# Sliding-window attention: score matmuls over 64 rows of the array, two heads beside each other, in place of 128-row matmuls over stacked high and low parts

## The chip, the cores and the metric

One core of one Trainium2 chip runs the whole program. The metric is device time in microseconds (us) of that core, from the program's start to its end. All times of the profile are microseconds unless a column says ns.

## The reference

The program computes a two-layer decoder trunk for 1024 tokens of width 1024. Layer 0 mixes tokens with a gated linear recurrence, layer 1 with sliding-window attention; each is followed by a gated feed-forward net with a short convolution. The change lies in the attention: 16 query heads and 4 key/value heads of width 64, a window of 128 tokens, a learned sink for each head and a relative-position bias. Cut to that:

```python
def swa_sink_mixer(h, k, v, w_q, sinks, bias, mask, w_out):
    q = (h @ w_q).reshape(B, nb, SW_WINDOW, SW_KV_HEADS, SW_GROUP, SW_HEAD_DIM)
    kk, vv = with_prev(k), with_prev(v)          # blocks [j-1, j]: 256 keys for 128 queries
    logits = jnp.einsum('bntgrd,bnsgd->bngrts', q, kk) * SW_HEAD_DIM ** -0.5
    logits = jnp.where(mask, logits + bias, -jnp.inf)
    m = jnp.maximum(logits.max(-1), sink)
    p = jnp.exp(logits - m[..., None])
    denom = p.sum(-1) + jnp.exp(sink - m)
    o = jnp.einsum('bngrts,bnsgd->bntgrd', p, vv)
    return (o / denom).reshape(B, S, D) @ w_out
```

The `einsum` of the third line, queries by keys over 64 numbers, is the operation whose form changes.

## The kernel before

**High and low parts.** Nearly every matmul works on numbers that are split in two: a high part (the value as the array's fast 32-bit format, `F32R`, holds it) and a low part (the value less the high part). A product is then three matmuls: high by high, high by low, low by high. `mm3` (L172 to L174) writes these three; with its column of `psmm` or `psax`, both in PSUM, it makes most of the program. ScalarE (ACT) makes a high part by a copy, VectorE (DVE) a low part by a subtraction.

**The attention stage.** It begins when the first layer's feed-forward net ends. `k_part` projects the shared keys, `v_part` the values. Heads are worked in eight pairs `c`; the two heads `e` of a pair belong to neighbouring key heads. `q_unit(c)` loads the query weights of a pair (through a ring of raw tiles, `load`, L138, and a ring of six slots of the tile `HL`), `q_proj` projects them in two halves of 512 tokens, and `q_split` takes each half out of PSUM, scaled by 0.125. `attend(c, bp, q)` then does four steps `bp` for a pair, each of two blocks `jj` of 128 queries and both heads: scores, mask and bias, softmax, transposes, values. That makes 32 calls.

**Scores before.** A head has width 64, half of the array's 128 rows. The kernel fills the rows with both parts. `K` holds for each head 64 rows of the high part and, in the other 64 partitions, its low part (`k_part` writes the low part across, L1140). The query's high part stands twice, in both halves of the partitions (tile `q`), and its low part once, with zeros in the other half (`QB`, in slot 5 of `HL`, whose zeros are set at L1307). One 128-row matmul of the doubled high part then gives high by high plus high by low, a second with the low part gives low by high: two matmuls for each head and block (L1208), eight in a call, each with 128x128 weights of its own and 256 columns of keys streamed (128 for the first block). They write `psax`, head 0 in one PSUM bank, head 1 in the other.

**The transfers.** ACT and DVE write the two parts into a raw tile (`place["ML"]`, L1191 and L1192), which is thereby taken out of the ring of three, and six DMAs on SyncE's queue (L1196) carry the 64-row halves to their places. There are 16 such halves, and so 96 DMAs, 64 into `q` and 32 into `HL`.

**Order.** In the attention, the order on TensorE (PE), ACT, DVE and GpSimd (POOL) is that of the code; the SyncE queue (SP) is filled by a scheduler. The main loop (L1325 to L1357) is a pipeline written by hand: in each turn PE does the scores of call n, the values product (L1251, L1253) and the transposes of earlier calls, and two pieces of the next pair's `q_proj` as filler. After them DVE and ACT work on softmax while PE goes on.

Of the kernel before, what the change touches and what calls it, by code (L numbers as in the profile page):

```python
# [10 lines left out]
F32 = mybir.dt.float32  # L11
F32R = mybir.dt.float32r
U8 = mybir.dt.uint8
AF = mybir.ActivationFunctionType
ALU = mybir.AluOpType

P = 128
# [68 lines left out]
def trunk(ctx: ExitStack, tc: tile.TileContext, a: dict, out: bass.AP):  # L86
    nc = tc.nc
# [38 lines left out]
    ring = {"hl": 4, "raw": 0}  # L126
    tail, place = {}, {}
# [4 lines left out]
    def hl_at(i):  # L132
        return HL[:, 2048 * i:2048 * (i + 1)].rearrange("p (h n) -> p h n", h=2)
# [2 lines left out]
        return hl_at(j // 2)[:, j % 2, :]  # L136

    def load(loads):  # L138
        raw = tail["raw"][ring["raw"] % len(tail["raw"])]
        ring["raw"] += 1  # L140
        for view, src in loads(raw):
            nc.sync.dma_start(view, src)
        return raw
# [54 lines left out]
    def split(hi, lo, src, eng=None):  # L198
        nc.scalar.copy(hi, src)  # L199
        return low_part(lo, src, hi, eng)  # L200

    def split_scaled(hi, lo, src, scale):
        nc.scalar.activation(hi, src, AF.Copy, scale=scale)
        nc.vector.scalar_tensor_tensor(lo, src, scale, hi.bitcast(F32), op0=ALU.mult, op1=ALU.subtract)
# [461 lines left out]
    with tc.tile_pool(name="t", bufs=1, reuse_waits="tile") as raws, hgrn_pool as hp:  # L666
# [40 lines left out]
        with tc.tile_pool(name="ep", bufs=1, reuse_waits="tile") as ep:  # L707
# [50 lines left out]
            ps = psmm()  # L758
# [315 lines left out]
        ps = psax()  # L1074
# [25 lines left out]
    with (tc.tile_pool(name="ta", bufs=1, reuse_waits="tile") as raws,  # L1100
          tc.tile_pool(name="at", bufs=1, reuse_waits="tile") as at):
        raw_tail(raws)
        K = at.tile([P, 2, 2, S], F32R, name="K")
        QB = [hl_at(5)[:, i, :].rearrange("p (e t) -> p e t", e=2) for i in range(2)]
        tri = at.tile([P, P], F32, name="tri")
        nc.scalar.dma_start(tri, a["tri"])
        sk = at.tile([P, 16], F32, name="sk")
# [23 lines left out]
        def k_part(half):  # L1131
            ts = slice(half * 512, (half + 1) * 512)
            for c in range(2):
                ps = psmm()
                proj_T(khl[c], half, ps)
                heads = [(slice(64 * e, 64 * e + 64), slice(64 - 64 * e, 128 - 64 * e)) for e in range(2)]
                for e, (es, os) in enumerate(heads):
                    nc.scalar.copy(K[es, c, e, ts], ps[es])
                for e, (es, os) in enumerate(heads):
                    nc.vector.tensor_tensor(K[os, c, e, ts], ps[es], K[es, c, e, ts].bitcast(F32), op=ALU.subtract)  # L1140


        def v_part(tp):
# [20 lines left out]
        def q_unit(c):  # L1164
            bias_load(c)
            pp, r = divmod(c, 4)
            ring["hl"] = (2, 3, 4, 0, 1, 2, 3, 4)[c]
            hl = unit(lambda t: [(t.rearrange("p (k g e) -> p k g e", k=KC, g=2)[:, :, g, :],
                                  wq[:, :, 8 * pp + 4 * g + r, :]) for g in range(2)], lows)
            return hl.rearrange("p h (k c) -> p h k c", k=KC)  # L1170

        def q_proj(hl):
            qs, done = [], []
            yield qs, done
            for half in range(2):
                q = at.tile([P, 2, 512], F32R, name="q", bufs=3), QB[half]
                qs.append(q)
                ps = psmm()
                for kc in range(KC):
                    mm3(ps, lambda i: hl[:, i, kc, :], lambda i: T[:, i, kc, half * 512:(half + 1) * 512],  # L1180
                        kc == 0, kc == KC - 1)
                    od.tick()
                    if kc % 2 == 1 and kc < KC - 1:
                        yield
                done.append((q, ps))
                yield

        def q_split(q, ps):
            qh, ql = q
            M, L = [place["ML"][:, 512 * i:512 * i + 512] for i in range(2)]  # L1190
            nc.scalar.activation(M.bitcast(F32R), ps, AF.Copy, scale=0.125)  # L1191
            nc.vector.scalar_tensor_tensor(L.bitcast(F32R), ps, 0.125, M, op0=ALU.mult, op1=ALU.subtract)  # L1192
            for e in range(2):
                es, os = slice(64 * e, 64 * e + 64), slice(64 - 64 * e, 128 - 64 * e)
                for dst, src in ((qh[es, e, :], M), (qh[os, e, :], M), (ql[es, e, :], L)):
                    nc.sync.dma_start(dst.bitcast(F32), src[es])  # L1196

        def attend(c, bp, q):
            pp, r = divmod(c, 4)
            ps = psax()  # L1200
            pv = ps.rearrange("p (e j s) -> p e j s", e=2, j=2)
            for jj in range(2):
                j = 2 * bp + jj
                lo = P if j == 0 else 0
                qs, ks = slice((j % 4) * P, (j % 4 + 1) * P), slice((j - 1) * P + lo, (j + 1) * P)
                for e in range(2):
                    for part in range(2):
                        nc.tensor.matmul(pv[:, e, jj, lo:], q[bp // 2][part][:, e, qs], K[:, pp, e, ks],  # L1208
                                         start=part == 0, stop=part == 1)
            XS = at.tile([P, 2, 2, 144], F32, name="X", bufs=4)  # L1210
            X, XS = XS[:, :, :, :P], XS[:, :, :, :P + 1]
            nc.scalar.copy(X, pv[:, :, :, P:])
            nc.gpsimd.tensor_copy(XS[:, :, :, P], sk[:, 8 * pp + r:8 * pp + r + 5:4].unsqueeze(2).to_broadcast([P, 2, 2]))
            yield
            j0 = 1 if bp == 0 else 0
            for e in range(2):
                nc.vector.copy_predicated(X[:, e, j0:, :], msk[:, 7 * BL:].unsqueeze(1).to_broadcast([P, 2 - j0, P]),
                                          pv[:, e, j0:, :P])
                if j0:
                    nc.gpsimd.affine_select(out=X[:, e, 0, :], in_=X[:, e, 0, :], compare_op=ALU.is_ge,  # L1220
                                            fill=NEG, base=0, pattern=[[-1, P]], channel_multiplier=1)
            bv = bfs[c]
            nc.gpsimd.tensor_tensor(X, X, bv.unsqueeze(2).to_broadcast([P, 2, 2, P]), op=ALU.add)
            yield
            nm = sm.tile([P, 2, 2], F32, name="nm")
            dn = sm.tile([P, 2, 2], F32, name="dn")
            nc.vector.tensor_reduce(nm, XS, axis=mybir.AxisListType.X, op=ALU.max, negate=True)
            for e in range(2):
                for jj in range(2):
                    nc.scalar.activation(XS[:, e, jj, :], XS[:, e, jj, :], AF.Exp, bias=nm[:, e, jj:jj + 1],  # L1230
                                         accum_out=dn[:, e, jj:jj + 1])
            yield
            nc.vector.reciprocal(dn, dn)
            nc.vector.tensor_tensor(X, X, dn.unsqueeze(3).to_broadcast([P, 2, 2, P]), op=ALU.mult)
            yield
            pt = psmm()
            for i in range(4):
                tr(pt[:, i * P:(i + 1) * P], X[:, i // 2, i % 2, :])
            yield
            W = W0 if bp % 2 else Y[:, NB - 1, :].rearrange("p (k g s) -> p k g s", k=2, g=4)  # L1240
            nc.vector.tensor_tensor(W[:, 0], pt.rearrange("p (g s) -> p g s", g=4),
                                    tri.unsqueeze(1).to_broadcast([P, 4, P]), op=ALU.mult)
            nc.scalar.copy(W[:, 1], pt.rearrange("p (g s) -> p g s", g=4))
            yield
            po = psmm()
            for jj in range(2):
                j = 2 * bp + jj
                for e in range(2):
                    kvc = (2 * pp + e) * 64
                    o = po[64 * e:64 * e + 64, jj * P:(jj + 1) * P]  # L1250
                    mm32(o, Vt[:, max(j - 1, 0), kvc:kvc + 64], W[:, 1, 2 * e + jj, :], stop=j == 0)  # L1251
                    if j:
                        mm32(o, Vd[:, j - 1, kvc:kvc + 64], W[:, 0, 2 * e + jj, :], start=False)  # L1253
            if c < 7:
                nc.scalar.copy(Y[:, c, bp * 256:(bp + 1) * 256], po[:, :256])
            else:
                ts = slice(bp * 256, (bp + 1) * 256)
                split(T[:, 0, c, ts], T[:, 1, c, ts], po[:, :256], lows)
            yield
# [34 lines left out]
        with tc.manual_schedule(engines={EN.PE, EN.Activation, EN.DVE, EN.Pool}):  # L1294
# [9 lines left out]
            hl = q_unit(0)  # L1304
            make_lows()
            k_part(1)
            for e in range(2):  # L1307
                nc.gpsimd.memset(hl_at(5).rearrange("p i (e t) -> p i e t", e=2)[64 - 64 * e:128 - 64 * e, :, e, :]
                                 .bitcast(F32), 0.0)
            g = q_proj(hl)  # L1310
            q, done = next(g)
            hl = q_unit(1)
            make_lows()
            place["ML"] = tail["raw"][ring["raw"] % 3]
            tail["raw"] = [t for t in tail["raw"] if t is not place["ML"]]
            for _ in g:
                while done:
                    q_split(*done.pop(0))
# [97 lines left out]
```

## Time and profile before

| | us |
|---|---|
| median of 3 runs | 2199.43 (2193.86 to 2200.97) |
| the profiled execution, its own time | 2199.59 |
| its span in the trace | 2197.8 |
| PE busy | 2156.2 (98%) |
| DVE busy | 1743.4 (79%) |
| ACT busy | 926.8 (42%) |

The profiled execution's own time is 1.8 us over its span, and 0.2 us over the median of the runs. A matmul's bar in the trace is longer than the time by which it delays the next: matmuls are pipelined, and 256 columns that show as 283 ns follow each other closer than that. So the distance from start to start is read here, not the bar. PEld are the weight loads, which run beside matmuls.

### The profile page before, as it was taken

Reading aid. Unit: us, or ns where it says so; the run is one execution under the profiler, and the core shown is the slowest. Engines: PE = TensorE matmul, PEld = TensorE weight load, DVE = VectorE, ACT = ScalarE, POOL = GpSimd, SP = SyncE. Lnnn points to the kernel's source line nnn. Section 1 sums busy time; section 2 is a strip of 40 time slices with the busy share of each in tenths; the row PEclk is TensorE's granted clock in tenths of the full one; section 3 lists DMA queues with packets and bytes.
Section 4 is the critical chain, followed back from the end, with each engine's and each line's share of the span. In section 5 each row is a group of like instructions: output and inputs, shape, how many; then the busy total and the mean of one; then the engine's idle time right before and its main releaser. Section 6 shows DMA issues by size and latency. Waiting matters only on the chain.

```text
span 2197.8 us, 33422 instructions
## 1 busy us (share of the span) xinstructions
PE 2156.2 (98%) x13135; PEld 1815.5 (83%) x13135; DVE 1743.4 (79%) x2295; ACT 926.8 (42%) x1577; POOL 187.3 (9%) x209
## 2 busy tenths in 40 slices
PE   8999999999999999999999999999999999999998
PEld 7888888978888888887888888878888888887887
DVE  3777665565789988888998766657899988889987
ACT  4333333332744443344344346655644444443431
POOL 0221111120100000000000122211000000000001
PEclk9999999999999999999999999999999999999999
DMA  5554443252222222238854354433123222259563
GB/s 198 193 192 173 154 173 116 64 126 90 87 84 86 85 82 87 86 103 268 281 169 133 105 145 108 111 118 118 68 96 106 86 77 77 78 168 318 187 212 135
DMA packets 239623, 293.68 MB, mean 134 GB/s; under 512 B 31513, under 2 KB 162282, under 8 KB 236650
## 3 DMA queue, kind: packets, MB, share of 16 engines
q1 hardware_dynamic: 236416, 289.12, 40.7%
q10 hardware_dynamic: 3050, 2.43, 0.9%
q8 instruction: 103, 1.69, 0.3%
q14 instruction: 54, 0.44, 0.1%
HBM read 213.90 MB, written 65.01 MB: 127 GB/s over the span
## 4 chain that ended last, share of the span: by engine, by line
PE 80%; DVE 10%; DMA 3%; ACT 3%; issue 2%; SPq 1%; POOL 1%; ACTq 0%; DVEq 0%; POOLq 0%
PE psmm L172 16%; PE psmm L173 16%; PE psmm L174 16%; PE psax L174 8%; PE psax L172 8%; PE psax L173 8%; PE psax L178 3%; DVE T L147 2%; PE psmm L178 1%; PE psax L1208 1%; PE psax L182 1%; ACT T L199 1%; ACT Y L247 1%; DVE Y L477 1%; DVE HL L147 1%
## 5 line engine op out<-in xcount | busy, mean ns | idle before, releaser
L172 PE MATMUL psmm<-T,HL 128*128 128x512 f32 x768 | 307.5, 400 | 0.0
L173 PE MATMUL psmm<-T,HL 128*128 128x512 f32 x768 | 300.0, 391 | 4.1 <-DVE T L147 2.8
L174 PE MATMUL psmm<-T,HL 128*128 128x512 f32 x768 | 300.1, 391 | 0.0
L477 DVE SCALAR_TENSOR_TENSOR Y<-Y,cwt 128x1023 f32<-128x1023 f32 (+1 forms) x176 | 225.1, 1279 | 39.1 <-ACT Y L475 38.8
L475 ACT ACTIVATE Y<-Y,cwt 128x1024 f32<-128x1024 f32 x88 | 108.9, 1238 | 257.2 <-DVE Y L464 254.1
L172 PE MATMUL psmm<-HL,T 128*128 128x256 f32 (+1 forms) x656 | 199.6, 304 | 1.2 <-ACT T L199 1.2
L173 PE MATMUL psmm<-HL,T 128*128 128x256 f32 (+1 forms) x656 | 195.0, 297 | 1.2 <-DVE HL L147 1.2
L174 PE MATMUL psmm<-HL,T 128*128 128x256 f32 (+1 forms) x656 | 195.0, 297 | 0.6 <-DVE T L147 0.5
L199 ACT CAST HL<-rx 128x1024 fp32r<-128x1024 f32 (+1 forms) x137 | 140.2, 1046 | 122.5 <-DMA rx<-in_ffn_w_in_dram 33.6
L147 DVE TENSOR_TENSOR HL<-rx,HL 128x1024 fp32r<-128x1024 f32 (+1 forms) x137 | 165.6, 1211 | 13.7 <-ACT HL L199 12.8
L174 PEld LDWEIGHTS psmm<-T,HL 128*128 128x128 f32 x768 | 144.5, 188 | 32.8 <-issue 1.6
L173 PEld LDWEIGHTS psmm<-T,HL 128*128 128x128 f32 x768 | 144.7, 188 | 31.1 <-DVE T L147 3.5
L172 PEld LDWEIGHTS psmm<-T,HL 128*128 128x128 f32 x768 | 144.4, 188 | 30.7 <-issue 1.6
L221 POOL TENSOR_TENSOR rs<-rs,nhalf 128x1 f32<-128x1 f32 x32 | 25.9, 812 | 1308.6 <-DVE rs L220 1308.4
L172 PE MATMUL psax<-T,HL 128*128 128x512 f32 x352 | 137.3, 390 | 0.0
L174 PE MATMUL psax<-T,HL 128*128 128x512 f32 x352 | 137.0, 389 | 0.0
L173 PE MATMUL psax<-T,HL 128*128 128x512 f32 x352 | 136.9, 389 | 0.0
L172 PEld LDWEIGHTS psmm<-HL,T 128*128 128x128 f32 x656 | 126.0, 192 | 7.8 <-issue 2.5
L173 PEld LDWEIGHTS psmm<-HL,T 128*128 128x128 f32 x656 | 126.1, 192 | 4.9 <-DVE HL L147 1.7
L174 PEld LDWEIGHTS psmm<-HL,T 128*128 128x128 f32 x656 | 126.0, 192 | 4.3 <-DVE T L147 1.1
L856 POOL TENSOR_TENSOR kp<-kp,tot 128x512 f32<-128x512 f32 x48 | 73.9, 1539 | 287.9 <-PE psax L178 148.0
L147 DVE TENSOR_TENSOR HL<-raw,HL 128x1024 fp32r<-128x1024 f32 x51 | 65.3, 1280 | 19.8 <-ACT HL L154 19.8
(297 smaller groups left out, 5262.4 us busy)
## 6 DMA issues: line engine op xcount, KB each, us to landing
rx<-in_ffn_w_in_dram SPq DMA_DIRECT2D x136, 256.0 KB, 3.2
rx<-gd SPq DMA_DIRECT2D x118, 256.0 KB, 3.6
Y<-in_ffn_w_out_dram SPq DMA_DIRECT2D x44, 512.0 KB, 6.4
bsd<-Y SPq DMA_DIRECT2D x22, 1024.0 KB, 4.8
gd<-Y SPq DMA_DIRECT2D x44, 512.0 KB, 2.6
rx<-in_ffn_w_out_dram SPq DMA_DIRECT2D x54, 256.0 KB, 3.9
R<-bsd SPq DMA_DIRECT2D x44, 256.0 KB, 4.3
Y<-in_ffn_w_in_dram SPq DMA_DIRECT2D x40, 256.0 KB, 3.1
```

The source lines that it names most:

```text
L147: make = lambda e: e.tensor_tensor(lo, src, hi.bitcast(F32), op=ALU.subtract)
L172: nc.tensor.matmul(ps, st(0), mv(0), start=start, stop=False)
L173: nc.tensor.matmul(ps, st(0), mv(1), start=False, stop=False)
L174: nc.tensor.matmul(ps, st(1), mv(0), start=False, stop=stop)
L178: nc.tensor.matmul(ps, lhsT, rhs, start=start, stop=stop, **kw)
L182: nc.tensor.transpose(ps, src, ident)
L199: nc.scalar.copy(hi, src)
L221: nc.gpsimd.tensor_tensor(rs, rs, nhalf, op=ALU.pow)
L247: nc.scalar.activation(hf[:, kc, :], ps[:, k * P:(k + 1) * P], AF.Identity, bias=shift, scale=scale)
L475: nc.scalar.activation(c, u, AF.Identity, bias=cwt[:, l, 3, ci:ci + 1], scale=cwt[:, l, 2, ci:ci + 1])
L477: nc.vector.scalar_tensor_tensor(c[:, sh:], u[:, :S - sh], cwt[:, l, 2 - sh, ci:ci + 1], c[:, sh:], op0=ALU.mult, op1=ALU.add)
L856: (nc.gpsimd if i else nc.vector).tensor_tensor(kv[:, :, 0, :], kv[:, :, 0, :], tv[:, :, 1:2].to_broadcast([P, nb, m]), op=ALU.mult)
```

## The change

Keys and queries are kept in plain tiles: `K[:, 0]` holds the high parts of both heads of a pair (64 partitions each), `K[:, 1]` the low parts, and the same holds for `q`. ACT and DVE write both tiles directly (`split`, L198; `split_scaled`, L202). The zeros, the place `ML` and the DMAs of L1196 are gone, slot 5 of `HL` takes part in the ring of query weights, and the raw ring has three tiles throughout. The scores are three matmuls of 64 rows for each head and block; the two heads stand one after the other in the order, head 0 in rows 0 to 63 of the array and head 1 in rows 64 to 127. A call has twelve matmuls of 64 rows by 128 columns for eight of 128 by 128. Instructions behind the attention are the same.

```diff
     def load(loads):
-        raw = tail["raw"][ring["raw"] % len(tail["raw"])]
+        raw = tail["raw"][ring["raw"] % 3]
...
-        QB = [hl_at(5)[:, i, :].rearrange("p (e t) -> p e t", e=2) for i in range(2)]
...
                 proj_T(khl[c], half, ps)
-                heads = [(slice(64 * e, 64 * e + 64), slice(64 - 64 * e, 128 - 64 * e)) for e in range(2)]
-                for e, (es, os) in enumerate(heads):
-                    nc.scalar.copy(K[es, c, e, ts], ps[es])
-                for e, (es, os) in enumerate(heads):
-                    nc.vector.tensor_tensor(K[os, c, e, ts], ps[es], K[es, c, e, ts].bitcast(F32), op=ALU.subtract)
+                split(K[:, 0, c, ts], K[:, 1, c, ts], ps)
...
-            ring["hl"] = (2, 3, 4, 0, 1, 2, 3, 4)[c]
+            ring["hl"] = (2, 3, 4, 5, 0, 1, 4, 5)[c]
...
-                q = at.tile([P, 2, 512], F32R, name="q", bufs=3), QB[half]
+                q = at.tile([P, 2, 512], F32R, name="q", bufs=3)
...
         def q_split(q, ps):
-            qh, ql = q
-            M, L = [place["ML"][:, 512 * i:512 * i + 512] for i in range(2)]
-            nc.scalar.activation(M.bitcast(F32R), ps, AF.Copy, scale=0.125)
-            nc.vector.scalar_tensor_tensor(L.bitcast(F32R), ps, 0.125, M, op0=ALU.mult, op1=ALU.subtract)
-            for e in range(2):
-                es, os = slice(64 * e, 64 * e + 64), slice(64 - 64 * e, 128 - 64 * e)
-                for dst, src in ((qh[es, e, :], M), (qh[os, e, :], M), (ql[es, e, :], L)):
-                    nc.sync.dma_start(dst.bitcast(F32), src[es])
+            split_scaled(q[:, 0], q[:, 1], ps, 0.125)
...
-                for e in range(2):
-                    for part in range(2):
-                        nc.tensor.matmul(pv[:, e, jj, lo:], q[bp // 2][part][:, e, qs], K[:, pp, e, ks],
-                                         start=part == 0, stop=part == 1)
+                for n, (i, k) in enumerate(((0, 0), (0, 1), (1, 0))):
+                    for e in range(2):
+                        es = slice(64 * e, 64 * e + 64)
+                        nc.tensor.matmul(pv[:, e, jj, lo:], q[bp // 2][es, i, qs], K[es, k, pp, ks],
+                                         start=n == 0, stop=n == 2)
...
-            for e in range(2):
-                nc.gpsimd.memset(hl_at(5).rearrange("p i (e t) -> p i e t", e=2)[64 - 64 * e:128 - 64 * e, :, e, :]
-                                 .bitcast(F32), 0.0)
...
-            place["ML"] = tail["raw"][ring["raw"] % 3]
-            tail["raw"] = [t for t in tail["raw"] if t is not place["ML"]]
```

On PE the first call of the attention stands so before (L172 and L174 are the filler; the eight rows between are the scores, `q` the doubled high part and `HL` the padded low part as weights):

```order
L174 MATMUL psmm<-T,HL 128x512
L1208 MATMUL psax<-K,q 128x128
L1208 MATMUL psax<-K,HL 128x128
L1208 MATMUL psax<-K,q 128x128
L1208 MATMUL psax<-K,HL 128x128
L1208 MATMUL psax<-K,q 128x256
L1208 MATMUL psax<-K,HL 128x256
L1208 MATMUL psax<-K,q 128x256
L1208 MATMUL psax<-K,HL 128x256
L172 MATMUL psmm<-T,HL 128x512
```

and so after:

```order
L173 MATMUL psmm<-T,HL 128x512
L174 MATMUL psmm<-T,HL 128x512
L1197 MATMUL psax<-K,q 128x128 x6
L1197 MATMUL psax<-K,q 128x256 x6
L172 MATMUL psmm<-T,HL 128x512
```

Between the same two filler matmuls stand twelve score matmuls in place of eight; nothing else on PE has moved.

On SP's queue the same part of the program, from the last spills of the residual stream (`h2d`) on, reads before (`raw` tiles take weights from memory, `bf` is the bias of a pair):

```order
L270 DMA h2d<-Y 128x1024 x2
L142 DMA raw_10081<-in_swa_w_q_dram 128x8x64 x3
L1196 DMA q<-raw_10082 64x512 x2
L1196 DMA HL<-raw_10082 64x512
L1196 DMA q<-raw_10082 64x512 x2
L1196 DMA HL<-raw_10082 64x512
L1159 DMA bf<-rbd 128x2x128
L1196 DMA q<-raw_10082 64x512 x2
L1196 DMA HL<-raw_10082 64x512
L1196 DMA q<-raw_10082 64x512 x2
L1196 DMA HL<-raw_10082 64x512
L142 DMA raw_10083<-in_swa_w_q_dram 128x8x64 x2
```

and after:

```order
L270 DMA h2d<-Y 128x1024 x3
L142 DMA raw_10082<-in_swa_w_q_dram 128x8x64 x2
L1154 DMA bf<-rbd 128x2x128
L142 DMA raw_10083<-in_swa_w_q_dram 128x8x64 x2
L1154 DMA bf<-rbd 128x2x128
L142 DMA raw_10081<-in_swa_w_q_dram 128x8x64 x2
```

The loads of weights and biases now follow each other directly, over three raw tiles, and no transfer waits for ACT and DVE between them.

## The prediction

> **What bounds the kernel now.** I read the page first, for which engine sets the time: its busy times, and the chain of work that ended last.
>
> ```profile
> span 2197.8 us, 33422 instructions
> PE 2156.2 (98%) x13135; PEld 1815.5 (83%) x13135; DVE 1743.4 (79%) x2295; ACT 926.8 (42%) x1577; POOL 187.3 (9%) x209
> PE 80%; DVE 10%; DMA 3%; ACT 3%; issue 2%; SPq 1%; POOL 1%; ACTq 0%; DVEq 0%; POOLq 0%
> ```
>
> TensorE is the bound. Matmul time added to its queue lengthens the run by as much, and time taken out shortens it. Next comes the stage that the change touches, in the view of busy time by stretches (columns: stretch, its length, busy time and count of PE, PEld, DVE, ACT, POOL, the granted clock, DMA share, GB/s):
>
> ```profile
> 1283.00:1465.00 182.00, 175.60 (x1264) 148.36 (x1263) 120.51 (x225) 115.57 (x380) 56.05 (x81) 1.00 0.43 104
> ```
>
> From the first score to the last call PE is busy for 175.6 of 182 us at full clock, DVE for 120.5. So the attention is bound by PE too, with at most 6.4 us of visible gaps. The groups by line and shape give the scores:
>
> ```profile
> L1208 PE MATMUL psax<-K,q 128*128 128x256 f32 x112 | 28.6, 286 | 0.7 <-DMA q<-raw 0.7
> L1208 PE MATMUL psax<-K,HL 128*128 128x256 f32 x112 | 28.2, 283 | 0.2 <-DMA HL<-raw 0.2
> L1208 PE MATMUL psax<-K,HL 128*128 128x128 f32 x16 | 4.4, 286 | 1.2 <-DMA HL<-raw 1.2
> L1208 PE MATMUL psax<-K,q 128*128 128x128 f32 x16 | 3.9, 254 | 1.6 <-DMA q<-raw 1.6
> ```
>
> These are 256 matmuls, 8 in each of 32 calls. Their 283 ns overlap, so the timeline of PE in an undisturbed call gives the price (columns: start, length, engine, line, operation):
>
> ```profile
> 1340.93 0.39 PE L174 MATMUL psmm<-T,HL 128*128 128x512 f32 x1
> 1341.16 0.28 PE L1208 MATMUL psax<-K,q 128*128 128x256 f32 x1
> 1341.27 0.28 PE L1208 MATMUL psax<-K,HL 128*128 128x256 f32 x1
> ...
> 1341.99 0.28 PE L1208 MATMUL psax<-K,HL 128*128 128x256 f32 x1
> 1342.20 0.45 PE L178 MATMUL psmm<-W,Vt 128*64 128x128 f32 x4
> 1342.47 0.40 PE L178 MATMUL psmm<-W,Vd 128*64 128x128 f32 x4
> 1342.69 0.44 PE L178 MATMUL psmm<-W,Vt 128*64 128x128 f32 x4
> 1342.91 0.44 PE L178 MATMUL psmm<-W,Vd 128*64 128x128 f32 x4
> ```
>
> First to eighth score is 1341.99 less 1341.16, 0.83 us over seven steps: a pitch of 0.119 us. The eight cost 0.95 us a call, and 32 calls 30.5 us.
>
> **The change part by part: the scores.** Twelve matmuls take the place of eight. Each streams the same 256 columns, over half the rows. What counts is whether the two heads' matmuls, in rows 0 to 63 and 64 to 127, run at once. No matmul of this trace uses such a tile. The bounds are the pitch of 0.119 for each of the twelve (1.43 us a call, 45.7 in all, 15.2 more than before) and 0.119 for each of the six pairs (0.71 a call, 22.8 in all, 7.6 less).
>
> Which end is nearer? The weight loads speak first, in a call whose first block streams 128 columns only (PE and PEld together):
>
> ```profile
> 1373.94 0.19 PEld L1208 LDWEIGHTS psax<-K,HL 128*128 128x128 f32 x1
> ...
> 1374.05 0.19 PEld L1208 LDWEIGHTS psax<-K,q 128*128 128x128 f32 x1
> ...
> 1374.16 0.19 PEld L1208 LDWEIGHTS psax<-K,HL 128*128 128x128 f32 x1
> ...
> 1374.33 0.33 PE L1208 MATMUL psax<-K,q 128*128 128x256 f32 x1
> ...
> 1374.50 0.28 PE L1208 MATMUL psax<-K,HL 128*128 128x256 f32 x1
> ```
>
> With only 128 columns to stream, matmuls come no faster than their loads, which start 0.11 us apart. So a load of 128 weight columns occupies 0.11 us, nearly the whole pitch of 0.119. A 64-row tile still has 128 weight columns. If loads of the two row halves take turns, twelve cost 12 x 0.11 = 1.32 us a call, 42.2 in all, 11.8 more than before, even if the streams overlap. The Trainium skill, "TensorE: Matmul & The Clock Gate", section "LDWEIGHTS (loading the stationary operand)", says that load time follows the columns and not the rows: 128 columns in about 107 ns; the loads 0.11 apart agree.
>
> Against this stand tiles that split the columns. The values product above uses 64-column tiles: 16 matmuls in 1342.20 to 1343.35, overlapping in pairs. And in the recurrence, by line and shape:
>
> ```profile
> L178 PE MATMUL psax<-qp,kp 128*32 128x32 f32 x1792 | 23.9, 199 | 0.9 <-DVE qp L854 0.8
> ```
>
> 1792 matmuls of 32 weight columns are busy for 23.9 us, 13 ns each. Column tiles run side by side, loads included. But they share out weight columns and output partitions, whereas two row tiles each need all 128 of both. The nearest row for a matmul with a 128-column load of its own is the score of today, so I take 0.119 each, one after the other: plus 15.2.
>
> **Changing the tile.** Row tiles come between filler matmuls of 128x128 and values in 64-column tiles. One change of tile exists today behind the scores: 1341.99 to 1342.20 is 0.21 us where 0.12 is the pitch, 0.09 more. The change adds one in front of the scores in each call: 32 x 0.09 = 2.9 us. Bounds: nothing, if only column tiles pay it, and half as much again (4.5), since the first matmuls after such a change are slower too (1342.20 to 1342.47 for four). A gain is out, as a change of tile was not there before. The Trainium skill, "TensorEngine Tiling (Array Packing)", section "Key Properties", says that a change of tiling mode drains TensorE; by that rule the 2.9 is real rather than nothing, as the gap of 0.21 behind the scores suggests.
>
> **The transfers.** What the 96 DMAs cost is in the view of their line (who waited, us, times):
>
> ```profile
> L1196 SPq DMA_DIRECT2D q<-raw x64: 461/588/1772, 1278.7 to 1449.0; - x64
> ...
>   ACT raw L1191: 5.2, 1
>   PE psax L1208: 3.7, 10
>   PEld psax L1208: 3.4, 6
> ...
> DMA to landing us min/median/max: 2.2/2.3/3.9
> ```
>
> PE's matmuls waited 3.7 us for them and its loads another 3.4 while bars of earlier matmuls still stood. So between 3.7 and 7.1 us of PE's time goes; I take the middle, 5.4. What is late next? In the first pair, ACT and DVE take the first half of `q` out of PSUM:
>
> ```profile
> 1278.09 0.60 ACT L1191 ACTIVATE raw<-psmm 128x512 fp32r<-128x512 f32 x1 [3.19 <-PE psmm L174]
> 1279.18 0.69 DVE L1192 SCALAR_TENSOR_TENSOR raw<-psmm,raw 128x512 fp32r<-128x512 f32 x1
> ...
> 1283.33 0.22 PE L1208 MATMUL psax<-K,q 128*128 128x128 f32 x1
> ```
>
> They end at 1279.87, 3.4 us ahead of the first score at 1283.33, and after the change this is all that a score waits for. In later pairs these two instructions keep their places in the queues. So nothing takes the place of that wait.
>
> A second wait hangs on the transfers less directly. Here are PE's waits in the stage, then ACT's timeline:
>
> ```profile
> PE psmm L178 <- ACT Y L1243: 2.2, 2, 1.6
> 1420.57 1.05 ACT L154 CAST HL<-raw 128x1024 fp32r<-128x1024 f32 x1 [4.94 <-DMA raw<-in_swa_w_out_dram]
> ```
>
> ACT stood 4.94 us before the cast of output weights, and PE lost 1.6 behind it. Those loads had two raw tiles and were issued between transfers in SP's queue. With three tiles and no transfers ahead they are issued a turn earlier. I count 1.6 gone, with nothing as the other bound. Waits together: minus 7.0, between minus 3.7 and minus 8.7.
>
> **The rest** costs PE nothing. ACT and DVE write keys as one instruction of 128 partitions for two of 64; query splits are the same two instructions with another target; POOL loses the zeros. ACT is at 115.6 and DVE at 120.5 of 182 us, so what hides these is PE's own work, and without that cover fewer instructions would only gain. Slot 5 of `HL` is reloaded in place of slot 0 for the fourth pair, long after the keys' weights in it were used.
>
> **The sum**, on the profiled execution's own 2199.59: plus 15.2, plus 2.9, minus 7.0 is plus 11.1, 2210.7. That execution lies 0.2 over the median of the runs, so I say 2210.5. The case's own range: 11.8 + 0 - 8.7 = plus 3.1 (2202.5) with loads as the limit, and 15.2 + 4.5 - 3.7 = plus 16.0 (2215.5) with most waits left.
>
> **The rivals.** *Heads side by side.* The two heads alternate in the order and write separate PSUM banks, and column tiles of this trace do overlap, with their loads. If row tiles do so as well, a pair takes 0.119: minus 7.6, plus 2.9, minus 7.0 is minus 11.7, 2187.7, between 2183.1 (no cost for the tile, all waits gone) and 2192.4. It decides where a pair takes less than 0.18 us: at 192 pairs, 34.6 us pay exactly for 30.5 before, less 2.9 for tiles, plus 7.0 of waits. Against it speaks that one load of 128 columns fills 0.11 us, so the pair needs two at once. The Trainium skill, "TensorE: Matmul & The Clock Gate", section "Part 3: Packing small matmuls — row/col tiling", sides with this rival: tiles in different row groups overlap, loads too, with 3.07 times the speed for four tiles of 32 rows. No row here shows it.
>
> *In between.* Loads overlap partly, and a pair takes about 0.18: about 2199.4, no change that can be seen.
>
> *Loads no longer hidden.* Where a load came late in the call above, a matmul took 1374.33 to 1374.50, 0.17 us. If every 64-row matmul pays that, a call is 2.04 us, 34.8 more in all; with 2.9 and minus 7.0 that is plus 30.7, 2230.1. Against it: each half has the other half's stream of 0.11 us to load under.
>
> **How the numbers follow.** One after the other gets 0.56, side by side 0.28, in between 0.08, loads in the open 0.08. A measurement of this kernel can tell about 0.3%, 6.6 us, from no change. One after the other falls below that with about a tenth of its chance (0.06); with most of the in-between case that makes 0.12 for the same. Side by side gives 0.28 for faster. What is left, 0.50 and the 0.08 of open loads and a little of in between, is 0.60 for slower. The range runs from 2185, inside the side-by-side case, to 2218, a little over the upper end of the likeliest, as a few waits might return. It leaves out open loads and the best of side by side, about 0.2. The likeliest case alone is 2202.5 to 2215.5.
>
> **What would show it.** Starts of successive scores 0.12 apart in the timeline, about 1.4 us a call, show the forecast; starts in close twos with 0.12 from two to two, about 0.7 us a call, show the first rival. A pitch of 0.11 names the loads, 0.17 open loads. The gap from the filler's last matmul to the first score should grow from 0.23 by about 0.09. No score should wait for a DMA, and ACT should not stand 5 us before a cast of output weights. A stretch from first to last score that is longer for waits on ACT or DVE, with scores at their pitch, would show my cover wrong. The forecast is wrong above all if two row tiles overlap.

## The result and the profile after

The changed kernel takes 2188.1 us (median of 6 runs, 2184.37 to 2191.94), the kernel before 2199.6 in the same series: a ratio of 0.9955, 95% interval 0.9944 to 0.9966, some 10 us less. The forecast was 2210.5 and slower; the first rival, heads side by side, had said 2187.7. The page of the changed kernel:

```profile
span 2185.6 us, 33447 instructions
PE 2149.7 (98%) x13263; PEld 1803.4 (83%) x13263; DVE 1739.9 (80%) x2291; ACT 924.5 (42%) x1573; POOL 183.2 (8%) x207
PE 82%; DVE 9%; ACT 3%; DMA 3%; issue 2%; POOL 1%; SPq 0%; ACTq 0%; DVEq 0%; POOLq 0%
```

TensorE (PE) is still the bound. It has 128 matmuls more and is busy for 6.5 us less. The groups of the scores, by line and shape (64*128 are rows and columns of the array):

```profile
L1197 PE MATMUL psax<-K,q 64*128 64x256 f32 x336 | 27.9, 294 | 0.0
L1197 PE MATMUL psax<-K,q 64*128 64x128 f32 x48 | 4.4, 289 | 0.0
```

384 matmuls cover 32.3 us in all, 0.084 us each, less than the 0.11 at which the loads of before stood apart: they overlap. The timeline of PE in one call shows how:

```profile
1339.21 0.39 PE L174 MATMUL psmm<-T,HL 128*128 128x512 f32 x1
1339.53 0.97 PE L1197 MATMUL psax<-K,q 64*128 64x256 f32 x12
1340.43 0.45 PE L178 MATMUL psmm<-W,Vt 128*64 128x128 f32 x4
```

Twelve scores end 0.97 us after the first began, bars and all. In the instructions' starts they come in twos 3 to 4 ns apart, from two to two 0.117 us. In a window of the first 0.07 us there are two:

```profile
1339.53 0.39 PE L1197 MATMUL psax<-K,q 64*128 64x256 f32 x2
```

From the last filler matmul to the values product is 1.22 us here (1339.21 to 1340.43) where 1.27 was before (1340.93 to 1342.20). So the scores themselves, with their changes of tile, bring only 0.03 to 0.05 us a call, 1.4 us in 32 calls. The rest is waits. This is all that PE waits for in the stage 1283 to 1465 of the changed kernel, by the view of waits:

```profile
PE psmm L178 <- ACT W L1232: 0.5, 1, 0.5
```

And the busy times of that stretch (columns as in the prediction):

```profile
1283.00:1465.00 182.00, 181.50 (x1444) 144.96 (x1443) 124.75 (x232) 120.05 (x385) 54.23 (x81) 1.00 0.13 38
```

PE is busy 181.5 of 182 us (175.6 before), and the DMA share fell from 0.43 to 0.13. The starts of PE's matmuls, one trace against the other, give the ledger: the changed run is 1.6 us late when the attention begins and 8.0 us early at 1520, so 9.6 us are gained there, about the ratio's 10. In starts, scores late for their queries make 5.8 of them, values products late for ScalarE 2.3, the scores 1.4. The spans differ by 12.2; the other 2.6 us are outside the attention, where the granted clock dipped for some microseconds in both runs. It stood at half for 16.6 us in all in the run of before and for 11.2 in the changed one, which is worth 2.7 us. The last number but two is the clock, here over one dip of each; the kernel before:

```profile
1990.00:2010.00 20.00, 17.42 (x64) 13.63 (x63) 18.22 (x17) 6.51 (x7) 0.00 (x0) 0.83 0.88 297
```

The changed kernel:

```profile
1030.00:1040.00 10.00, 8.82 (x30) 6.88 (x31) 9.60 (x9) 3.52 (x4) 0.00 (x0) 0.83 0.87 289
```

### The profile page after: what moved, and what is told of

Same layout as the page of the kernel before. It is cut to its first block, busy times and chain, and to the rows that moved or that the text cites. A ratio compares the mean times of both kernels' runs of the same rounds, so it can differ in the third digit from the quotient of the medians.

```text
span 2185.6 us, 33447 instructions
## 1 busy us (share of the span) xinstructions
PE 2149.7 (98%) x13263; PEld 1803.4 (83%) x13263; DVE 1739.9 (80%) x2291; ACT 924.5 (42%) x1573; POOL 183.2 (8%) x207
## 4 chain that ended last, share of the span: by engine, by line
PE 82%; DVE 9%; ACT 3%; DMA 3%; issue 2%; POOL 1%; SPq 0%; ACTq 0%; DVEq 0%; POOLq 0%
PE psmm L172 17%; PE psmm L173 17%; PE psmm L174 16%; PE psax L172 8%; PE psax L173 8%; PE psax L174 8%; PE psax L178 3%; PE psmm L178 1%; PE psax L1197 1%; DVE T L147 1%; PE psax L182 1%; DVE Y L477 1%; DVE HL L147 1%; DMA rx<-in_ffn_w_in_dram 1%; ACT Y L247 1%
## 5 line engine op out<-in xcount | busy, mean ns | idle before, releaser
L172 PE MATMUL psmm<-T,HL 128*128 128x512 f32 x768 | 307.5, 400 | 0.0
L174 PE MATMUL psmm<-T,HL 128*128 128x512 f32 x768 | 299.8, 390 | 0.0
L172 PE MATMUL psmm<-HL,T 128*128 128x256 f32 (+1 forms) x656 | 199.8, 305 | 1.9 <-ACT T L199 1.7
L174 PE MATMUL psmm<-HL,T 128*128 128x256 f32 (+1 forms) x656 | 195.2, 297 | 1.4 <-DVE T L147 1.4
L174 PEld LDWEIGHTS psmm<-T,HL 128*128 128x128 f32 x768 | 144.2, 188 | 32.4 <-issue 1.4
L172 PEld LDWEIGHTS psmm<-T,HL 128*128 128x128 f32 x768 | 144.4, 188 | 30.5 <-issue 1.2
L172 PE MATMUL psax<-T,HL 128*128 128x512 f32 x352 | 137.4, 390 | 0.0
L174 PE MATMUL psax<-T,HL 128*128 128x512 f32 x352 | 137.1, 390 | 0.0
L172 PEld LDWEIGHTS psmm<-HL,T 128*128 128x128 f32 x656 | 126.1, 192 | 8.7 <-issue 2.5
L174 PEld LDWEIGHTS psmm<-HL,T 128*128 128x128 f32 x656 | 126.0, 192 | 5.2 <-DVE T L147 1.9
```

The source lines that it names most:

```text
L172: nc.tensor.matmul(ps, st(0), mv(0), start=start, stop=False)
L174: nc.tensor.matmul(ps, st(1), mv(0), start=False, stop=stop)
```

## The experiments

Each is timed beside the kernel before. With each time stands the stage's own length in the profile: from the last matmul ahead of the first score to the first transposing matmul behind the attention (`psmm<-ident,Y`, L182). It leaves out what the clock does elsewhere. It is 231.8 us before and 222.8 in all three profiles of the changed kernel. Two theories stood against each other. *Side by side*: the row halves of the array work at once, a change of tile costs some 0.2 us, and waits for transfers are gone. *Only the waits*: row tiles as such neither help nor hurt.

**Both heads in the same rows.** In the changed kernel:

```diff
-                        es = slice(64 * e, 64 * e + 64)
+                        es = slice(0, 64)
```

> Both heads' score matmuls take their operands from partitions 0 to 63, so that head 1 is computed from head 0's queries and keys; nothing else differs from the changed kernel. Theory 'side by side' (the two row halves of the array work at once, and that is why the scores got no dearer): in the same rows the pairs fall apart, starts 0.12 us apart in place of twos 0.003 apart, six more steps of 0.117 us in each of 32 calls, plus 22.5 us: about 2210.6. Rival 'only the waits' (the gain is the vanished waits for transfers, and the row tiles themselves neither help nor hurt): within 3 us of 2188. Rival 'loads take turns': a pitch of 0.11 a matmul, plus 20.

2211.3 us, ratio 1.0063 (1.0049 to 1.0076), stage 245.4. One call of it on PE:

```profile
1338.40 0.39 PE L174 MATMUL psmm<-T,HL 128*128 128x512 f32 x1
1338.72 1.68 PE L1197 MATMUL psax<-K,q 64*128 64x256 f32 x12
```

The same twelve matmuls take 1.68 us in place of 0.97, one every 0.12. That is about the forecast of 2210.5 (13.7 us over the kernel before of its series, where 11.1 was forecast), met by a kernel in which the heads can't overlap: its price was right, its premise not. The overlap is worth 24 us by the medians, 22.6 in the stage.

**The order of the heads.**

```diff
-                for n, (i, k) in enumerate(((0, 0), (0, 1), (1, 0))):
-                    for e in range(2):
-                        es = slice(64 * e, 64 * e + 64)
+                for e in range(2):
+                    es = slice(64 * e, 64 * e + 64)
+                    for n, (i, k) in enumerate(((0, 0), (0, 1), (1, 0))):
```

> The changed kernel with the order of the score loops turned: three matmuls of head 0, then three of head 1, for each block. Theory 'a queue for each tile' (a matmul for the idle row half starts past those that wait for the other half): starts still in twos, time within 2 us of 2188. Rival 'strictly in order': of each block's six matmuls only the third and fourth overlap, a block takes five steps in place of three, so about four more steps of 0.117 us in each of 32 calls, plus 15 us: about 2203.

2187.7 us, ratio 0.9957 (0.9944 to 0.9969), stage 223.0: no difference.

```profile
1340.76 0.39 PE L174 MATMUL psmm<-T,HL 128*128 128x512 f32 x1
1341.08 0.98 PE L1197 MATMUL psax<-K,q 64*128 64x256 f32 x12
```

Twelve in 0.98 us: starts still come in twos, 10 ns apart, though three matmuls of one head stand before those of the other. The records do not name the head of a matmul, but two in the same rows stood 0.12 apart in the run above, so the two of a pair are of different heads: a matmul for the idle half goes past at least two that wait for the busy one.

**The 128-row matmuls without transfers.** In the kernel before, `q_split` writes with ScalarE (four instructions of 64 partitions) and VectorE (two), three raw tiles:

```diff
+                nc.scalar.activation(qh[es, e, :], ps[es], AF.Copy, scale=0.125)
+                nc.scalar.activation(qh[os, e, :], ps[es], AF.Copy, scale=0.125)
+                nc.vector.scalar_tensor_tensor(ql[es, e, :], ps[es], 0.125, qh[es, e, :].bitcast(F32),
+                                               op0=ALU.mult, op1=ALU.subtract)
...
-                    nc.sync.dma_start(dst.bitcast(F32), src[es])
```

> The kernel before with its 128-row matmuls, its doubled high part and padded low part, but ScalarE and VectorE write the query parts to their places, across partitions, and no DMA does; the raw ring has three tiles. ScalarE has four instructions of 64 partitions for one of 128, VectorE two for one. Theory 'side by side with dear tile changes' says that the vanished waits are about 8 us of the gain in the attention and the scores 1.5: about 2191.5, with no score waiting for a DMA. Rival 'the row tiles bring it' (waits are refilled by something else): 2196 to 2199. ScalarE's extra 29 us, at 116 of 182 us busy today, may take back a few us if it comes to bound a turn.

2197.1 us, ratio 0.9996 (0.9988 to 1.0005), stage 231.9. The forecast of 2191.5 was a miss: ScalarE's extra work, which the expectation had named as a caution, took back all of the gain. PE's waits in the stage:

```profile
PE psmm L178 <- ACT W L1244: 5.9, 7, 1.7
PE psmm L174 <- DVE T L147: 1.9, 1, 1.9
```

Its busy times:

```profile
1283.00:1465.00 182.00, 173.91 (x1263) 147.49 (x1262) 132.41 (x245) 141.04 (x419) 62.90 (x81) 1.00 0.12 34
```

No score waits for a DMA, but ScalarE has 141.0 us of work in the stage for 115.6, and the values products wait for it instead. So this run did not tell the theories apart.

**The row tiles with transfers.** In the changed kernel the two parts go through a raw tile, taken out of the ring as before, and four DMAs a half:

```diff
-            split_scaled(q[:, 0], q[:, 1], ps, 0.125)
+            M, L = [place["ML"][:, 512 * i:512 * i + 512] for i in range(2)]
+            nc.scalar.activation(M.bitcast(F32R), ps, AF.Copy, scale=0.125)
+            nc.vector.scalar_tensor_tensor(L.bitcast(F32R), ps, 0.125, M, op0=ALU.mult, op1=ALU.subtract)
+            for e in range(2):
+                es = slice(64 * e, 64 * e + 64)
+                for dst, src in ((q[es, 0], M), (q[es, 1], L)):
+                    nc.sync.dma_start(dst.bitcast(F32), src[es])
```

> The changed kernel with its row tiles, but the query parts again go through a raw tile taken out of the ring and by DMA to their place, four DMAs of 64 partitions a half in place of six. If the waits for transfers make most of the gain: PE waits 4 to 8 us for DMAs again, time 2193 to 2197. If the row tiles make it: within 2 us of 2188, or at most 2190.

2189.1 us, ratio 0.9968 (0.9956 to 0.9981), stage 223.4. The expectation that waits return was wrong. Who waited for the DMAs of that line:

```profile
L1190 SPq DMA_DIRECT2D q<-raw x64: 461/564/1832, 1282.0 to 1443.4; - x64
...
  PEld psax L1203: 0.4, 1
  PE psax L1203: 0.2, 1
```

64 transfers cost 0.2 us of waits where 96 had cost 3.7; in starts, scores are 0.6 us late once, where 5.8 were lost before. So transfers as such are not late, and neither is the ring of two raw tiles at fault. ScalarE still stood 3.6 us for output weights, but no values product was late for it by more than the 0.5 of the changed kernel. On SP's queue a half takes four DMAs in place of six. The place of the low part differs too, a buffer of `q` in place of slot 5 of `HL`; the next run keeps that slot.

**The 128-row matmuls with two transfers.** In the kernel before, ScalarE and VectorE write in place, and only the doubled high part crosses:

```diff
+                nc.scalar.activation(qh[es, e, :], ps[es], AF.Copy, scale=0.125)
+                nc.vector.scalar_tensor_tensor(ql[es, e, :], ps[es], 0.125, qh[es, e, :].bitcast(F32),
+                                               op0=ALU.mult, op1=ALU.subtract)
+                nc.sync.dma_start(qh[os, e, :].bitcast(F32), qh[es, e, :].bitcast(F32))
```

> The kernel before with its 128-row matmuls, but ScalarE and VectorE write the query parts that stay in their partitions directly, and two DMAs a half in place of six carry the high part across; three raw tiles. ScalarE gets about 10 us more work in 182. Theory 'the waits were six DMA issues of 0.6 us one behind the other on SP's queue and a landing of 2.3': with two the scores no longer wait, minus 5 to 8 from 2198, so 2190 to 2193, and the rest of the gain of the changed kernel is 1.5 us of scores. Rival 'any transfer is late': 2196 to 2198, scores still wait for DMAs. Rival 'ScalarE takes it back': no score waits for a DMA, but values products wait for ScalarE by some us.

2190.9 us, ratio 0.9975 (0.9964 to 0.9985), stage 225.2, and no score waits for a DMA. SP's timeline of the kernel before shows what the six did in the second pair:

```profile
1304.04 1.11 SPq L1196 DMA_DIRECT2D q<-raw  x2
1305.25 0.54 SPq L1196 DMA_DIRECT2D HL<-raw  x1
1305.84 1.24 SPq L1196 DMA_DIRECT2D q<-raw  x2
1307.12 0.59 SPq L1196 DMA_DIRECT2D HL<-raw  x1
```

and PE's the scores of that call:

```profile
1307.67 0.22 PE L1208 MATMUL psax<-K,q 128*128 128x128 f32 x1
...
1309.45 0.33 PE L1208 MATMUL psax<-K,HL 128*128 128x128 f32 x1 [0.26 <-DMA HL<-raw]
```

The six are issued one after the other over 3.7 us. The last goes out at 1307.12, and with the 2.3 us to landing that the prediction quoted it is there at 1309.4; the score that needs it started at 1309.45, 1.8 us after its call began. So 6.6 of the 9.0 us that the change gains in the stage can be had without row tiles (5.5 of 10 by the ratios), and a half of a query projection could afford four issues, not six.

**One more change of tile.** The scores' second block comes behind the values product (in the main loop one more `stage(it)` behind `stage(prev[0])`):

```diff
                                          start=n == 0, stop=n == 2)
+                if jj == 0:
+                    yield
```

> The changed kernel with one more change of tile in a turn: the scores of the first block, then the values product of an earlier call (64-column tiles), then the scores of the second block, then transposes. The same instructions otherwise; 29 of 32 turns have a values product between. Theory 'a change of tile costs 0.2 us' (the gap in front of the first pair, 0.32 in place of 0.23, and the second pair, 0.22 behind the first in place of 0.117): plus 29 x 0.2 = 5.8, about 2194. Rival 'only the drain of 0.09': plus 2.6, about 2190.5. Rival 'no cost of its own' : within 1 us of 2188.

2193.9 us, ratio 0.9980 (0.9971 to 0.9989), stage 228.2: 5.5 to 6.6 us over the changed kernel by ratio and by medians (2187.3 in a later series), 5.4 in the stage. 29 changes of 0.2 us are 5.8.

**Two calls a turn.** If a change of tile is dear, half of them should be a gain. The loop runs over 16 turns; each does the scores of two calls (24 matmuls), the values products of two, eight transposes, four pieces of filler:

```diff
+        def attend2(c, half, q):
+            its = [attend(c, 2 * half + b, q) for b in range(2)]
+            for _ in range(7):
+                for it in its:
+                    next(it)
+                yield
```

> The changed kernel with its main loop in 16 turns of two calls each: 24 score matmuls, then both values products, then eight transposes, then four pieces of filler. The same matmuls with half the changes of tile; the chain from scores to transposes now has one turn of some 10 us in place of two of 5. Theory 'a change of tile costs 0.2 us in front of the scores and about 0.25 in all behind them': 16 turns save 16 x 0.45 = 7.2 us, about 2181, if softmax still ends before its transposes. Rival 'only the scores' 0.2': about 2185. Rival 'the shorter pipeline waits': transposes or values products wait for VectorE and ScalarE, 2188 or over.

2187.3 us, ratio 0.9951 (0.9938 to 0.9964), stage 221.1, no faster than the changed kernel. But its eleven steady turns took 9.94 us each, where two turns of the changed kernel take 10.53, and turns 13 and 14 (of 0 to 15) took 13.8 and 13.7. PE's waits there:

```profile
PE psmm L182 <- DVE q L204: 4.0, 2, 2.0
```

In turn 13 four casts, 4 us of work, stood ahead of the query split on ScalarE, VectorE's low part of the query waited for it, and the transposes behind that waited 2.0 us. Nearly as much again went to the clock: behind each of the two waits it was granted at 0.83 over 10 us (1419 to 1429 and 1433 to 1443), which is 1.7 us each. No other run here shows a dip in the stage.

**The same, with that work spread**, and the two values products in one PSUM tile:

> The loop of two calls a turn, with the work that ScalarE and VectorE do beside it spread: query split first, casts of finished heads behind the weight copies and their low parts behind the softmax's reductions, one unit of output weights a turn, and the second output row begun two pieces later. In the loop of two calls before, 12 steady turns were 9.95 us against 10.57 for two turns of the changed kernel, and turns 13 and 14 took 13.8 each. If the two long turns were ScalarE's and VectorE's queues alone, they shrink to 10 to 11 and the time is 2178 to 2182. If the shorter pipeline is the cause, they stay long: 2186 to 2188.

2190.9 us, ratio 0.9975 (0.9965 to 0.9984), stage 226.7. The two long turns fell to 10.8 and 11.4, as expected, but nearly every turn had a new wait, made by the shared tile:

```profile
PE psmm L178 <- ACT Y L1246: 7.3, 14, 1.3
```

The changed kernel beside it:

> The changed kernel once more, on the same chip and in the same rounds as the loop of two calls with the spread work, so that the two can be compared: 2186 to 2190 by the runs so far.

2186.7 us, ratio 0.9962 (0.9950 to 0.9975).

**The same, each product in its own PSUM tile:**

```diff
-            if bp % 2 == 0:
-                place["po"] = psmm()
-            po = place["po"][:, 256 * (bp % 2):256 * (bp % 2) + 256]
+            po = psmm()
```

> The loop of two calls a turn with the spread work, but each call's values product has a PSUM tile of its own again. With the shared tile the second product waited for ScalarE's copy of the first, 14 times for 7.3 us in all; turns 13 and 14 had come down to 10.8 and 11.4 us. Theory: the changes of tile that are saved show once nothing waits, turns of 9.95 us, 2181 to 2184. Rival: with output rows holding two of four PSUM tiles, the last turns wait for as much, 2186 or over.

2179.3 us, ratio 0.9913 (0.9900 to 0.9927), stage 214.0, a little under the 2181 to 2184 expected. One wait is left, and a turn reads so on PE (filler left out):

```profile
PE psmm L182 <- DVE T L147: 1.4, 1, 1.4
```

```profile
1375.79 1.69 PE L1197 MATMUL psax<-K,q 64*128 64x256 f32 x24
1377.40 0.45 PE L178 MATMUL psmm<-Y,Vt 128*64 128x128 f32 x4
...
1379.35 1.09 PE L182 MATMUL psmm<-ident,X 128*128 128x128 f32 x8
...
1385.85 0.33 PE L1197 MATMUL psax<-K,q 64*128 64x128 f32 x2
```

24 scores to the values product take 1.61 us, where two calls of the changed kernel take twice 0.90. The changed kernel beside it:

> The changed kernel on the same chip and in the same rounds, for comparison with the loop of two calls: 2186 to 2190.

2187.3 us, ratio 0.9952 (0.9938 to 0.9966). The loop of two calls is faster than both kernels, by 8 us over the changed one with the same matmuls. In the starts of the stage PE goes from one tile shape to another 50 times in place of 99, and the stage is 8.8 us shorter in spite of the wait of 1.4: some 0.2 us for each change saved.

## Why the prediction was wrong

**The step that failed** is "Which end is nearer?". It took the 128-row score as "the nearest row for a matmul with a 128-column load of its own" and put twelve one after the other, plus 15.2. Loads of two row halves do not take turns: with the heads in separate rows the twelve take 0.97 us, in the same rows 1.68. So the term of plus 15.2 was in truth about minus 7.6 (a pair at 0.117), and the kernel got faster and not slower. The row that should have decided was there and was argued away: column tiles in the trace overlapped, loads included. That row tiles share columns and output partitions was a reason without a row behind it. The rule of the Trainium skill that the prediction had named ("TensorE: Matmul & The Clock Gate", section "Part 3: Packing small matmuls — row/col tiling"), that tiles in different row groups overlap, holds here: starts 3 to 4 ns apart.

**The rival's terms.** Its total, 2187.7, was met (2188.1), its parts less so. A pair at 0.119 for minus 7.6 was right: 0.117. The change of tile was mis-sized: 0.09 us a call was only the gap in front of the first pair, which grew from 0.23 to 0.32 (1339.21 to 1339.53). The second pair then comes 0.22 behind the first in place of 0.117, another 0.11. Together it is 0.2 us, 6.3 in 32 calls in place of 2.9 and over the bound of 4.5. One more change a turn (plus 5.4 in the stage for 29) and half as many of all changes (minus 8.8) bear that out. Against minus 7.6, the scores thus kept 1.4. That the total came out so close is luck in part: a tile term 3.4 too small and waits 1.1 too small offset each other in part, and the medians here differ by 11.5 us where the ratio says 10. Two of the recorded sums are off by 0.1 and 0.2 us (11.8 for 11.7, 2192.4 for 2192.6), which changes nothing.

**The waits** were close: minus 7.0 forecast, 5.8 at scores and 2.3 at values products found. "So nothing takes the place of that wait" held, and output weights no longer hold up ScalarE. Why the transfers were late the prediction did not say: by SP's timeline and the runs with four and two DMAs a half, it was the count of issues on one queue.

**"The rest costs PE nothing"** held, since no other wait in the stage is over 0.5 us.

## What to carry to other kernels

Two matmuls of 64 rows, in different halves of the array, cost one here; their outputs lay in different PSUM banks, and whether that is needed was not tried. So contraction over 64 numbers needs no stacking to fill the rows, and nothing need be moved for it. What it costs is the change of tile, some 0.2 us for each here: gather work of one tile shape, as long as the engines behind keep up and each product has its own PSUM tile. And where a small tile arrives late, count the DMA issues ahead of it on its queue before blaming the transfer.

## What the runs showed of the hardware

- Two row tiles run past each other: with three matmuls of one head ahead of three of the other, starts still come in twos, 10 ns apart.
- Weight loads of two row tiles run at once: twelve loads of 128 columns fit in 0.77 us, though single ones stand 0.11 apart:

```profile
1339.53 0.77 PEld L1197 LDWEIGHTS psax<-K,q 64*128 64x128 f32 x12 [0.35 <-issue]
```

- That row shows, too, what a change of tile is. The first load starts 0.32 us behind the last filler matmul and together with the first score (both at 1339.53). In the kernel before, with no change of shape there, the load started 0.22 us ahead of its score (1340.94 for 1341.16). So the first load is not hidden. The first two scores show as 0.38 us where later ones show as 0.28, and the second pair is late by 0.11, the size of one load. That it is this load was not tried.
